# The opening stage of a hybrid encoder step: norm_pre behind the transposes for two tiles, POOL and DVE shares moved, a written order of squares and splits

## The chip, the core and the metric

The kernel runs on one core of a Trainium2 chip. The core has five engines with instruction streams of their own: TensorE (PE in the profile; its weight loads are listed as PEld), VectorE (DVE), ScalarE (ACT), GpSimd (POOL) and SyncE (SP, which here only issues DMAs). The metric is the device time of one execution in microseconds (us); lower is better. The time before is 2414.46 us, the median of three runs (2413.88 to 2417.59).

## The reference

One layer of a streaming encoder: RMSNorm, one combined input projection, two groups of attention heads, per-head norms and gates, one output projection, and a second RMSNorm. It is computed for 1024 prompt frames and for 8 x 16 sample frames (128 rows). What matters for the change is the start:

```python
def rms_norm(x, g):
    xf = x.astype(jnp.float32)
    y = xf * lax.rsqrt(jnp.mean(xf * xf, axis=-1, keepdims=True) + EPS)
    return (y * g.astype(jnp.float32)).astype(x.dtype)

...
    h = rms_norm(xp, norm_pre[l])
    q_sb, k_sb, v_sb, gate_sb, q_r, k_r, v_r, gate_r = project(h, w_in[l], pos_p)
```

`x` has 2048 columns, `w_in` is 2048 x 8192, all in float32. `rms_norm` multiplies each row by a number of its own (1/rms) and each column by `norm_pre`.

## The kernel before

The frames are tiles of 128 rows. Group 0 holds the prompt tiles 0 to 3 and the sample tile (the "tile 4" of the text, loaded as `x_sample`), group 1 the prompt tiles 4 to 7. For the projections the normalised `h` must lie transposed (its 2048 columns on partitions, as 16 blocks of 128) and as two float32r parts whose sum is `h`: the high part `mh` and the low part `ml`. A product is then three matmuls: high by high, low by high, high by low. The weights are split in the same way (`wr` into `wh` and `wl`).

The opening stage brings group 0 into that form. For a tile it does this:

- SP loads the rows, `xt`, 128 x 2048 (`load_x`, line 355).
- ACT squares the row and adds it up (`sq`, line 361); ACT and DVE make 1/rms of it (`inv_rms`, lines 137 to 143: `p0v`, `p0r`, `p0u`, six operations on 128x1 of which three have two inputs in SBUF).
- DVE multiplies the identity by 1/rms, row by row: the diagonal matrix `dg` (line 388).
- `xt` is multiplied by `norm_pre` in place, in eight pieces of 256 columns (line 391): on DVE for tile 0 and tile 4, on POOL for the tiles 1 to 3. `gpre` is `norm_pre` copied to all 128 partitions by two DMAs of 512 KB.
- PE multiplies each block of `xt` by `dg`, which transposes and scales it at once (line 371), four blocks (a quarter) to a PSUM buffer `p0t`, of which there are four. Tile 4 is scaled on DVE instead (line 395) and transposed with the identity (line 369).
- ACT copies the quarter into `mh` (line 129) and DVE subtracts for `ml` (line 130).

After tile 1 the first weight column (`load_w`: four chunks, each loaded, split and multiplied) is applied to the 256 columns of tiles 0 and 1 (`products`, line 226, into the first bank of `acc`); after tile 4 to the other 384 columns (second bank). Then come the projection of the next column (again line 226) and `project_rows` (line 285, into `accn`), which is the first work of PE in which the two kernels do not differ any more. Beside these products a background job (`stage_rest`) loads, squares, scales (line 428 on DVE, 128x2048) and transposes the tiles of group 1.

A scheduler sets the order of instructions on each engine when the program is built; the source gives it dependencies, and here and there an order only (`tc.add_manual_dep` with SCHED_ONLY, `tc.issue_after`). Each engine then runs its stream in that order, and an instruction that waits holds up those behind it.

## Time and profile before

| what | value |
|---|---|
| median of 3 runs | 2414.46 us |
| the profiled execution | 2413.81 us, span 2412.1 us |
| PE busy over the span | 2338.0 us (97%) |
| DVE, ACT, POOL busy over the span | 1255.4, 913.6, 647.9 us |
| DVE `ml` from PSUM, 128x512 | 20 by 678 ns |
| ACT square of a tile, 128x2048 | 9 by 1909 ns |
| POOL multiply by `gpre`, 128x256 | 24 by 824 ns |

All times of the trace are from the start of the span. In a row of the timeline stand the start, the time to the end of the last instruction, the engine, the line of the source, the operation, its tiles (written <- read) and its count; in brackets how long the engine had been idle and what ended that. A mean or a busy time of PE is no measure of its speed, since its matmuls overlap; the distance from start to start is. Clock means the share of PE's full clock that was granted. Lines are those of the kernel before; in the kernel after the same operations have other line numbers.

### The profile page before, as it was taken

Reading aid. Unit: us, or ns where it says so; the run is one execution under the profiler, and the core shown is the slowest. Engines: PE = TensorE matmul, PEld = TensorE weight load, DVE = VectorE, ACT = ScalarE, POOL = GpSimd, SP = SyncE. Lnnn points to the kernel's source line nnn. Section 1 sums busy time; section 2 is a strip of 40 time slices with the busy share of each in tenths; the row PEclk is TensorE's granted clock in tenths of the full one; section 3 lists DMA queues with packets and bytes.
Section 4 is the critical chain, followed back from the end, with each engine's and each line's share of the span. In section 5 each row is a group of like instructions: output and inputs, shape, how many; then the busy total and the mean of one; then the engine's idle time right before and its main releaser. Section 6 shows DMA issues by size and latency. Waiting matters only on the chain.

```text
span 2412.1 us, 40463 instructions
## 1 busy us (share of the span) xinstructions
PE 2338.0 (97%) x14832; PEld 2099.1 (87%) x14832; DVE 1255.4 (52%) x2434; ACT 913.6 (38%) x1929; POOL 647.9 (27%) x1029
## 2 busy tenths in 40 slices
PE   7999999999999999998999999999999998999998
PEld 7998999999999999997778888889888877878787
DVE  7245445455554555455545555554545564564544
ACT  6323333333333333324333334333443343444343
POOL 3144353444444353443202112120120211000000
PEclk9999999999999999999999999999999999999999
DMA  7669779797978788797965565665556566765554
GB/s 243 167 129 218 157 172 195 174 199 160 197 170 189 174 180 189 186 190 186 198 169 146 140 158 152 148 146 153 139 150 152 154 167 165 233 210 182 190 183 130
DMA packets 674888, 418.67 MB, mean 174 GB/s; under 512 B 224512, under 2 KB 619776, under 8 KB 672256
## 3 DMA queue, kind: packets, MB, share of 16 engines
q1 hardware_dynamic: 524272, 285.99, 48.3%
q0 software_dynamic: 32256, 71.36, 13.5%
q10 hardware_dynamic: 118160, 58.74, 8.8%
q8 instruction: 116, 1.90, 0.3%
q14 instruction: 84, 0.69, 0.1%
HBM read 336.24 MB, written 79.69 MB: 172 GB/s over the span
## 4 chain that ended last, share of the span: by engine, by line
PE 84%; DMA 8%; DVE 4%; ACT 1%; issue 1%; POOL 1%; SPq 0%; DVEq 0%; ACTq 0%; POOLq 0%
PE acc L226 45%; PE accn L285 17%; PE a L993 3%; PE a L994 3%; PE a L992 3%; DMA mr<-s_y 3%; PE pa L615 3%; PE z L585 2%; DMA wr<-w_in 2%; PE zc L658 1%; PE pd L725 1%; DMA wr<-w_out 1%; DVE ml L130 1%; DVE out L1054 1%; DVE wl L130 1%
## 5 line engine op out<-in xcount | busy, mean ns | idle before, releaser
L226 PE MATMUL acc<-mh,wh 128*128 128x256 f32 (+2 forms) x2304 | 664.0, 341 | 6.4 <-ACT wh L129 4.7
L226 PE MATMUL acc<-ml,wh 128*128 128x384 f32 (+2 forms) x2304 | 665.4, 342 | 0.0
L226 PE MATMUL acc<-mh,wl 128*128 128x256 f32 (+2 forms) x2304 | 659.2, 339 | 0.9 <-DVE wl L130 0.7
L130 DVE TENSOR_TENSOR wl<-wr,wh 128x512 fp32r<-128x512 f32 (+1 forms) x576 | 393.4, 688 | 504.6 <-ACT wh L129 502.3
L129 ACT ACTIVATE wh<-wr 128x512 fp32r<-128x512 f32 (+1 forms) x576 | 356.1, 624 | 685.4 <-PE acc L226 255.0
L226 PEld LDWEIGHTS acc<-mh,wh 128*128 128x128 f32 x2304 | 420.8, 189 | 41.9 <-ACT wh L129 5.6
L226 PEld LDWEIGHTS acc<-ml,wh 128*128 128x128 f32 x2304 | 422.6, 189 | 33.4 <-issue 6.2
L226 PEld LDWEIGHTS acc<-mh,wl 128*128 128x128 f32 x2304 | 424.2, 189 | 31.0 <-DVE wl L130 2.6
L642 POOL DMA_DIRECT2D kc<-cache_sb_k x512 | 331.3, 653 | 366.2 <-DVE kcT L680 201.5
L285 PE MATMUL accn<-whn,mh 128*128 128x256 f32 x1152 | 330.1, 287 | 2.7 <-DVE rg L312 2.7
L285 PE MATMUL accn<-wln,mh 128*128 128x256 f32 x1152 | 326.8, 284 | 2.2 <-DVE wln L130 2.2
L285 PE MATMUL accn<-whn,ml 128*128 128x256 f32 x1152 | 326.6, 284 | 0.0
L285 PEld LDWEIGHTS accn<-whn,mh 128*128 128x128 f32 x1152 | 221.3, 192 | 12.3 <-issue 7.7
L993 PE MATMUL a<-wl,mh 128*128 128x512 f32 (+1 forms) x576 | 221.6, 385 | 7.1 <-DVE wl L130 7.0
L285 PEld LDWEIGHTS accn<-wln,mh 128*128 128x128 f32 x1152 | 221.8, 193 | 2.8 <-DVE wln L130 2.4
L285 PEld LDWEIGHTS accn<-whn,ml 128*128 128x128 f32 x1152 | 221.6, 192 | 0.0
L992 PE MATMUL a<-wh,mh 128*128 128x512 f32 (+1 forms) x576 | 219.9, 384 | 0.8 <-DVE so L618 0.5
L994 PE MATMUL a<-wh,ml 128*128 128x512 f32 (+1 forms) x576 | 220.6, 383 | 0.0
L993 PEld LDWEIGHTS a<-wl,mh 128*128 128x128 f32 x576 | 109.4, 190 | 29.8 <-DVE wl L130 9.0
L130 DVE TENSOR_TENSOR wln<-wrn,whn 128x512 fp32r<-128x512 f32 x128 | 86.7, 688 | 88.9 <-ACT whn L129 88.9
L478 POOL DMA_DIRECT2D be<-s_be x128 | 94.1, 741 | 131.0 <-DMA s_be<-be 116.5
L503 POOL TENSOR_SCALAR_AFFINE_SELECT kp<-kp 128x128 f32<-128x128 f32 x40 | 14.5, 362 | 426.0 <-ACT kp L497 425.9
(189 smaller groups left out, 2680.5 us busy)
## 6 DMA issues: line engine op xcount, KB each, us to landing
wr<-w_in SPq DMA_DIRECT2D x384, 256.0 KB, 4.2
wr<-w_out SPq DMA_DIRECT2D x184, 256.0 KB, 3.6
wrn<-w_in SPq DMA_DIRECT2D x128, 256.0 KB, 3.2
kc<-cache_sb_k POOLq DMA_DIRECT2D x512, 64.0 KB, 5.1
vc<-cache_sb_v SPq DMA_DIRECT2D x64, 512.0 KB, 9.1
xt<-x_prompt SPq DMA_DIRECT2D x8, 1024.0 KB, 6.0
xr<-x_prompt SPq DMA_DIRECT2D x8, 1024.0 KB, 6.5
out<-out ACTq DMA_DIRECT2D x12, 512.0 KB, 2.9
```

Of the source, the lines that this page charges most:

```text
L129: nc.scalar.activation(hi, src, AF.Copy)
L130: nc.vector.tensor_tensor(lo, src, hi.bitcast(F32), ALU.subtract)
L226: last = nc.tensor.matmul(a[:, :m], lhs[:, j, :], rhs[w][:, j, o : o + m], start=(w == 0 and j == 0 and n == 0), stop=(w == KT // WQ - 1 a ...
L285: anchor[0] = nc.tensor.matmul(a, lhs[q][:, jj, ts], rhs[:, j, :], start=(w == 0 and j == 0 and n == 0 and t % 2 == 0), stop=(w == KT // 2 ...
L478: q.dma_start(raw[32 * i : 32 * i + 32, :].rearrange("p (k a) -> p k a", a=32), s[:, :, 32 * i : 32 * i + 32].rearrange("k (j b) a -> b (k ...
L585: nc.tensor.matmul(z[:, :c], q2[a][:, i * P : (i + 1) * P], k2[b][:, s : s + c], start=(m == 0), stop=(m == 2),)
L615: nc.tensor.matmul(po[:, :P], at[:, j, :], vn[:, j, :], start=(j == 0), stop=(j == t))
L642: nc.gpsimd.dma_start(kc[32 * i : 32 * i + 32, :].rearrange("p (k d) -> p k d", d=32), cache_k[0, 2 * c + j, s * 512 : (s + 1) * 512, h, 3 ...
L658: mm = nc.tensor.matmul(z[r, :], qp[:, j, r], ready[2 * j + c // 2][:, c % 2, :], start=(j == 0), stop=(j == 1),)
L992: nc.tensor.matmul(a[:, :width], hi[q][:, j, ts], wh, start=(k == 0), stop=False)
L993: nc.tensor.matmul(a[:, :width], hi[q][:, j, ts], wl, start=False, stop=False)
L994: nc.tensor.matmul(a[:, :width], lo[q][:, j, ts], wh, start=False, stop=(k == KT - 1))
```

## The change

- Tiles 0 and 1 are no longer multiplied by `norm_pre` before the transposes. `norm_pre` is also loaded as 16 rows of 128 (`grow`, on ACT's DMA queue), transposed by PE and copied to `gcol`, 128x16. After a transpose the columns of `x` lie on partitions, so `gcol` is a factor per partition: DVE multiplies the quarter out of PSUM by it into an SBUF tile `xg`, and the split reads `xg`.
- The low parts of the first six quarters (all of tile 0, two of tile 1) are subtracted on POOL, the other two of tile 1 on DVE.
- The tiles 2 and 3 are still multiplied by `gpre` on POOL, tile 4 on DVE. Tile 4 gets a `dg` as well, and no scaling on DVE.
- PE starts with twenty matmuls of a constant tile (`busy`), whose results nobody reads.
- `x` of tile 1 is loaded ahead of `gpre`.
- Squares, multiplies, weight splits and the first transposes of a tile are told not to be placed ahead of named instructions of PE. Tile 4's second to fourth quarter are transposed between the products of the second bank, a quarter ahead of each fourth of the products.

```diff
+        low.tensor_tensor(lo, src, hi.bitcast(F32), ALU.subtract)
...
-            loaded = [load_x(tiles[0])]
+            busy = p0s.tile([P, P], F32, name="busy")
+            nc.vector.memset(busy, 1.37)
+            grow = p0s.tile([KT, P], F32, name="grow")
+            nc.scalar.dma_start(grow, norm_pre[0].rearrange("(k p) -> k p", p=P))
+            loaded = [load_x(tiles[0]), load_x(tiles[1])]
+            pt = p0p.tile([P, 4, P], F32, name="p0t", tag="p0t")
+            for j in range(WARM):
+                nc.tensor.matmul(pt[:, j % 4, :], busy, busy, start=True, stop=True)
...
+            gcol = p0s.tile([P, KT], F32, name="gcol")
+            pt = p0p.tile([P, 4, P], F32, name="p0t", tag="p0t")
+            nc.tensor.transpose(pt[:, 0, :KT], grow, ident[:KT, :KT])
+            nc.vector.tensor_copy(gcol, pt[:, 0, :KT])
...
+            def stats(i, other=None):
+                with tc.high_priority():
+                    rstd = mean_square(loaded[i], other)
                     dg = p0.tile([P, P], F32, name="dg", tag="dg")
                     nc.vector.tensor_scalar(dg, ident, rstd, None, ALU.mult)
-                for c in range(PRE_CUT):
...
+                for c in range(8 if i > 1 else 0):
+                    cs = slice(c * D // 8, (c + 1) * D // 8)
+                    eng = nc.gpsimd if i < 4 else nc.vector
+                    ins = eng.tensor_tensor(loaded[i][:, cs], loaded[i][:, cs], gpre[:, cs], ALU.mult)
+                    behind(ins, other)
...
+            def turn_quarter(i, q, dg, other=None):
+                cs = slice(i * P, (i + 1) * P)
+                pt = turn(q, loaded[i], dg, other)
+                hi, lo = mov[0][q][:, :, cs], mov[1][q][:, :, cs]
+                if i > 1:
+                    split(hi, lo, pt)
+                    return
+                xg = p0.tile([P, 4, P], F32, name="xg", tag="xg", bufs=3)
+                nc.vector.tensor_tensor(
+                    xg, pt, gcol[:, 4 * q : 4 * q + 4].unsqueeze(2).to_broadcast([P, 4, P]), ALU.mult
+                )
+                split(hi, lo, xg, None, nc.gpsimd if 4 * i + q < 6 else nc.vector)
+
+            scales = [stats(0), stats(1)]
+            for q in quarters:
+                turn_quarter(0, q, scales[0])
+            raw = [fetch_w(col(4, 0), q) for q in quarters]
+            loaded += [load_x(t) for t in tiles[2:]]
+            w4 = []
+            for q in quarters:
+                turn_quarter(1, q, scales[1])
+                w4.append((q, *split_w(raw[q], anchor[0])))
+            scales.append(stats(2, anchor[0]))
+            acc = acc_banks(g0)
+            for n, w in enumerate(w4):
+                last = products(mov, acc[:1], g0["pieces"][:1], *w)
+                if n == 1:
+                    scales.append(stats(3, last))
+            for i in (2, 3):
+                for q in quarters:
+                    turn_quarter(i, q, scales[i], last if q == 0 else None)
+                if i == 2:
+                    scales.append(stats(4, anchor[0]))
+            for q in quarters:
+                turn_quarter(4, q, scales[4], last if q else None)
+                last = products(mov, acc[1:], g0["pieces"][1:], *w4[q])
```

What this makes of the order shows on three engines. POOL, from its start to its first cache loads (`kc`), before; `ident` is the identity, and the count at the end is that of equal instructions:

```order
masks.py:197 MEMSET ident 128x128
masks.py:199 ISA
masks.py:199 AFFINE_SELECT ident<-ident 128x128
L391 TENSOR_TENSOR xt<-xt,gpre 128x256 x24
L642 DMA kc<-cache_sb_k 32x16x32 x29
```

The same place of POOL after; `ml_142` to `ml_148` are the low parts of the four quarters, first of tile 0, then of tile 1:

```order
L134 TENSOR_TENSOR ml_142<-xg,mh_141 128x4x128
L134 TENSOR_TENSOR ml_144<-xg,mh_143 128x4x128
L134 TENSOR_TENSOR ml_146<-xg,mh_145 128x4x128
L134 TENSOR_TENSOR ml_148<-xg,mh_147 128x4x128
L134 TENSOR_TENSOR ml_142<-xg,mh_141 128x4x128
L134 TENSOR_TENSOR ml_144<-xg,mh_143 128x4x128
L421 TENSOR_TENSOR xt<-xt,gpre 128x256 x16
```

Tile 1's eight multiplies are gone from POOL; six subtractions of twice the width stand ahead of the sixteen multiplies of tiles 2 and 3.

DVE before, where the low parts of tile 3 (the first `ml_142` to `ml_148` here) and of tile 4 (the second set) are made; `sw` and `rq` belong to the first product bank, L395 is tile 4's scaling:

```order
L391 TENSOR_TENSOR xt<-xt,gpre 128x256 x2
L130 TENSOR_TENSOR ml_142<-p0t,mh_141 128x4x128
L395 TENSOR_SCALAR xt<-xt,p0r 128x2048
L321 TENSOR_TENSOR sw<-sw,sinT 128x256
L322 TENSOR_TENSOR rq<-acc_322,cosT 128x256
L130 TENSOR_TENSOR ml_144<-p0t,mh_143 128x4x128
L130 TENSOR_TENSOR ml_146<-p0t,mh_145 128x4x128
L130 TENSOR_TENSOR ml_148<-p0t,mh_147 128x4x128
L130 TENSOR_TENSOR ml_142<-p0t,mh_141 128x4x128
L130 TENSOR_TENSOR ml_144<-p0t,mh_143 128x4x128
```

The same place of DVE after; the L421 row is the last of tile 4's eight multiplies, and the second `ml_142` is the first subtraction of tile 4:

```order
L417 TENSOR_SCALAR dg<-ident,p0r 128x128
L421 TENSOR_TENSOR xt<-xt,gpre 128x256 x2
L134 TENSOR_TENSOR ml_142<-p0t,mh_141 128x4x128
L134 TENSOR_TENSOR ml_144<-p0t,mh_143 128x4x128
L134 TENSOR_TENSOR ml_146<-p0t,mh_145 128x4x128
L134 TENSOR_TENSOR ml_148<-p0t,mh_147 128x4x128
L134 TENSOR_TENSOR ml_142<-p0t,mh_141 128x4x128
```

And what follows there, up to the second subtraction of tile 4; L478 is the scaling of a tile of group 1 (L428 before):

```order
L141 TENSOR_SCALAR p0v<-ssq 128x1
L143 RECIPROCAL p0r<-p0r 128x1
L144 TENSOR_TENSOR p0u<-p0r 128x1
L145 TENSOR_TENSOR p0u<-p0u,p0v 128x1
L146 TENSOR_SCALAR p0u<-p0u 128x1
L147 TENSOR_TENSOR p0r<-p0r,p0u 128x1
L478 SCALAR_TENSOR_TENSOR xt<-xt,p0r,gpre 128x2048
L141 TENSOR_SCALAR p0v<-ssq 128x1
L134 TENSOR_TENSOR ml_144<-p0t,mh_143 128x4x128
```

All eight multiplies of tile 4 now stand ahead of tile 3's four subtractions, and between the first and the second subtraction of tile 4 stand a scale chain and a scaling of group 1.

PE before, from the end of the first product bank (`acc_322`) to the start of the second (`acc_323`):

```order
L226 MATMUL acc_322<-mh_147,wl 128x256
L371 MATMUL p0t<-dg,xt 128x128 x32
L369 MATMUL p0t<-ident,xt 128x128 x8
L226 MATMUL acc_323<-mh_141,wh 128x384
L369 MATMUL p0t<-ident,xt 128x128 x8
L226 MATMUL acc_323<-ml_142,wh 128x384
```

PE after, some rows on, between the first and the second fourth of the second bank (now `acc_352`; `acc_599` and `acc_600` are the two banks of the next weight column):

```order
L235 MATMUL acc_352<-ml_142,wh 128x384
L235 MATMUL acc_352<-mh_141,wl 128x384
L389 MATMUL p0t<-dg,xt 128x128 x4
L235 MATMUL acc_352<-mh_143,wh 128x384
L235 MATMUL acc_599<-mh_141,wh 128x256
L235 MATMUL acc_600<-mh_141,wh 128x384
L235 MATMUL acc_352<-ml_144,wh 128x384
```

Tile 4's quarters moved in between the products, as float32 matmuls by `dg` and no longer as transposes with the identity.

More of the change, by code (lines that the diff above doesn't have):

```diff
@@ L27 @@
 WQ = 4
-PRE_POOL = (1, 2, 3)
-PRE_DIAG = (0, 1, 2, 3)
-PRE_CUT = 8
-PRE_G = 2
 D_REST = 8
+WARM = 20
 KC_AHEAD = 2
@@ L126, in tile_hybrid_step, with split @@
     ]
-    def split(hi, lo, src):
-        nc.scalar.activation(hi, src, AF.Copy)
-        nc.vector.tensor_tensor(lo, src, hi.bitcast(F32), ALU.subtract)
+    def split(hi, lo, src, behind=None, low=nc.vector):
+        ins = nc.scalar.activation(hi, src, AF.Copy)
+        if behind is not None:
+            tc.add_manual_dep(
+                ins.ins,
+                behind.ins.name,
+                mybir.DependencyInfo(mybir.DependencyClass.NoSync, mybir.DependencyReason.SCHED_ONLY),
+                reason="not placed ahead of the transposes",
+            )
+        low.tensor_tensor(lo, src, hi.bitcast(F32), ALU.subtract)
     def inv_rms(pool, ssq, n, name):
@@ L370, in turn @@
                     else:
-                        nc.tensor.matmul(pt[:, j, :], blk, scale, start=True, stop=True)
+                        anchor[0] = nc.tensor.matmul(pt[:, j, :], blk, scale, start=True, stop=True)
+                        if j == 0:
+                            behind(anchor[0], other)
                 return pt
             tiles = g0["tiles"]
-            loaded = [load_x(tiles[0])]
+            busy = p0s.tile([P, P], F32, name="busy")
+            nc.vector.memset(busy, 1.37)
@@ L402, in tile_hybrid_step @@
+                return dg
+            def turn_quarter(i, q, dg, other=None):
                 cs = slice(i * P, (i + 1) * P)
-                for q in range(KT // 4):
-                    pt = turn(q, loaded[i], scales[i])
-                    split(mov[0][q][:, :, cs], mov[1][q][:, :, cs], pt)
-                if i == 1:
-                    w4 = list(load_w(col(4, 0)))
-                    loaded += [load_x(t) for t in tiles[3:]]
-                    acc = acc_banks(g0)
-                    for w in w4:
-                        products(mov, acc[:1], g0["pieces"][:1], *w)
@@ L412, in tile_hybrid_step @@
-            for w in w4:
-                last = products(mov, acc[1:], g0["pieces"][1:], *w)
+                pt = turn(q, loaded[i], dg, other)
[6 more added lines that the diff above has]
+                    xg, pt, gcol[:, 4 * q : 4 * q + 4].unsqueeze(2).to_broadcast([P, 4, P]), ALU.mult
+                )
```

58 lines of the change are left out of this document (27 added, 31 removed).

## The prediction

> **What bounds the kernel now.** I read the page's busy line and chain first, to see which engine a microsecond has to be taken from.
>
> ```profile
> PE 2338.0 (97%) x14832; PEld 2099.1 (87%) x14832; DVE 1255.4 (52%) x2434; ACT 913.6 (38%) x1929; POOL 647.9 (27%) x1029
> ...
> PE 84%; DMA 8%; DVE 4%; ACT 1%; issue 1%; POOL 1%; SPq 0%; DVEq 0%; ACTq 0%; POOLq 0%
> ```
>
> TensorE (PE) is the bound, so a change in the opening stage is worth what it changes in PE's waiting and in PE's own work there. The second view, the waits of the first 45 us, says where PE waits today (and POOL, in the first row); the columns are the total, how often, and the longest.
>
> ```profile
> POOL xt L391 <- ACT sq L361: 13.7, 2, 12.3
> PE p0t L371 <- DVE dg L388: 10.6, 1, 10.6
> ...
> PE p0t L371 <- DVE p0v L137: 2.2, 1, 2.2
> ...
> PE p0t L371 <- issue: 1.5, 1, 1.5
> ...
> PE p0t L369 <- DVE xt L395: 1.0, 1, 1.0
> ...
> PE p0t L369 <- DVE ml L130: 0.5, 1, 0.5
> ```
>
> Third, PE in order of time. A start is followed by the time to the last end. One fp32 matmul is two passes, so a tile's sixteen are "x32"; the transposes of the sample tile with the identity are one pass each (x4 a quarter).
>
> ```profile
> 10.56 6.05 PE L371 MATMUL p0t<-dg,xt 128*128 128x128 f32 x32 [10.56 <-DVE dg L388]
> 18.84 5.35 PE L371 MATMUL p0t<-dg,xt 128*128 128x128 f32 x32 [2.22 <-DVE p0v L137]
> 23.94 0.36 PE L226 MATMUL acc<-mh,wh 128*128 128x256 f32 x1
> ...
> 30.39 3.74 PE L371 MATMUL p0t<-dg,xt 128*128 128x128 f32 x32
> 35.66 3.81 PE L371 MATMUL p0t<-dg,xt 128*128 128x128 f32 x32 [1.53 <-issue]
> 40.42 0.63 PE L369 MATMUL p0t<-ident,xt 128*128 128x128 f32 x4 [0.96 <-DVE xt L395]
> 41.59 0.66 PE L369 MATMUL p0t<-ident,xt 128*128 128x128 f32 x4 [0.55 <-DVE ml L130]
> 42.01 0.43 PE L226 MATMUL acc<-mh,wh 128*128 128x384 f32 x1
> 42.27 1.18 PE L369 MATMUL p0t<-ident,xt 128*128 128x128 f32 x8
> 43.39 0.44 PE L226 MATMUL acc<-ml,wh 128*128 128x384 f32 x1
> ...
> 67.53 0.28 PE L285 MATMUL accn<-whn,mh 128*128 128x256 f32 x1
> ```
>
> From 43.39 PE is fed without a gap. My yardstick is the last row: the first L285 product at 67.53. Behind it every engine has the same instructions in the same order before and after the change, so what that row moves by, the end moves by.
>
> Fourth, the clock. The columns are the stretch, its length, busy time of PE, PEld, DVE, ACT, POOL, and the granted clock.
>
> ```profile
> 10.00:15.00 5.00, 4.44 (x21) 4.44 (x22) 2.09 (x7) 3.17 (x5) 1.35 (x2) 1.00 1.05 381
> ...
> 15.20:18.60 3.40, 1.42 (x12) 1.22 (x11) 2.68 (x8) 2.84 (x4) 3.40 (x6) 1.00 1.14 368
> 18.60:22.10 3.50, 3.26 (x15) 3.29 (x16) 2.84 (x6) 1.91 (x5) 3.50 (x5) 0.51 0.99 399
> ```
>
> A stretch in which PE worked 1.42 of 3.40 us is followed by one at half clock. A pass is 0.211 us at the slow rate (4.44/21) and 0.117 at the full one (3.74/32).
>
> **The change, step by step.** I follow PE and keep account of its lead over the kernel before.
>
> *Tile 0.* Its scale `dg` no longer shares VectorE (DVE) with eight multiplies.
>
> ```profile
> 5.76 1.91 ACT L361 ACTIVATE sq<-xt 128x2048 f32<-128x2048 f32 x1 [3.45 <-DMA xt<-x_prompt]
> ...
> 8.22 0.16 DVE L139 RECIPROCAL p0r<-p0r 128x1 f32<-128x1 f32 x1
> ...
> 10.23 0.28 DVE L388 TENSOR_SCALAR dg<-ident,p0r 128x128 f32<-128x128 f32 x1
> ...
> 11.57 1.91 ACT L361 ACTIVATE sq<-xt 128x2048 f32<-128x2048 f32 x1 [3.38 <-DMA xt<-x_prompt]
> ...
> 29.07 0.16 DVE L139 RECIPROCAL p0r<-p0r 128x1 f32<-128x1 f32 x1 [0.27 <-ACT p0r L138]
> 29.27 0.16 DVE L140 TENSOR_TENSOR p0u<-p0r 128x1 f32<-128x1 f32 x1
> 29.47 0.59 DVE L141 TENSOR_TENSOR p0u<-p0u,p0v 128x1 f32<-128x1 f32 x1
> ...
> 30.28 0.47 DVE L143 TENSOR_TENSOR p0r<-p0r,p0u 128x1 f32<-128x1 f32 x1
> 30.79 0.72 DVE L388 TENSOR_SCALAR dg<-ident,p0r 128x128 f32<-128x128 f32 x1
> ```
>
> Undisturbed steps follow each other by 0.20 us (29.07 to 29.27). From the reciprocal at 8.22 that is four steps, a 0.15 copy of `gcol`, and the 0.28 of `dg`: ready at 9.45 and not 10.51. The twenty warm matmuls are 40 passes, 4.7 to 8.4 us from about 1.2 us on, inside PE's first wait of 10.6: they cost nothing. With the clock up the tile takes 3.74 and not 6.05: done at 13.3, before at 16.6. **Lead 3.3** (1.1 if the clock is not up).
>
> *Tile 1.* Its load is issued ahead of the 1 MB of `gpre`; at the 381 GB/s above that brings its square from 11.57 to about 8.9. But its scale chain now runs while POOL does the low-part subtractions of tile 0. In the rows at 29.47, 30.28 and 30.79, three steps that cost 0.16, 0.16 and 0.28 alone took 0.59, 0.47 and 0.72 beside POOL's multiplies. POOL's instructions:
>
> ```profile
> 13.65 11.94 POOL L391 TENSOR_TENSOR xt<-xt,gpre 128x256 f32<-128x256 f32 x16 [12.28 <-ACT sq L361]
> ...
> 27.01 6.85 POOL L391 TENSOR_TENSOR xt<-xt,gpre 128x256 f32<-128x256 f32 x8 [1.43 <-ACT sq L361]
> ```
>
> ```profile
> L391 POOL TENSOR_TENSOR xt<-xt,gpre 128x256 f32<-128x256 f32 x24 | 18.8, 824 | 13.7 <-ACT sq L361 13.7
> ...
> L1052 POOL TENSOR_TENSOR out<-out,xr 128x512 f32<-128x512 f32 x3 | 5.2, 1738 | 120.8 <-ACT out L1051 120.8
> ```
>
> A 128x512 subtraction is not in the trace on POOL: two multiplies of 11.94/16 give 1.49, the 128x512 addition gives 1.74; I take 1.45, since the low end is the same operation on the same engine. A DVE step caught behind one waits about twice what it waited behind a multiply: four steps lose 2 to 4 us, three 0.69 multiplies by `gcol` stand between them, and from the step at 11.1 `dg` comes at about 16.4 (14.5 to 17.5). Transposes from 16.4, not 18.84; after 3.1 us of idling I charge the half clock again (5.35, as before): done at 21.8 against 24.2. **Lead 2.4.** The 48 products follow as they do now (6.4 us): **lead 2.0** at their end, 28.3.
>
> [...]
>
> *Tile 2 and 3.* This is where I see the lead go. POOL now has six subtractions (about 8.7 us) ahead of the sixteen multiplies; the fifth and sixth wait for tile 1's transposes (18 to 20) plus its `gcol` multiply and split, so POOL is through at about 23. Then it waits for ACT's square of tile 2, which is held behind tile 1's transposes and stands behind four weight splits: 22.9 to 25. Eight multiplies at 6.85 (the row at 27.01): tile 2 is multiplied at 31.8, before at 25.6. PE finishes tile 2 at about 33.0, before at 34.1: **lead 1.1**. Eight more, 6.0 to 6.85: tile 3 is multiplied at 38.2, before at 33.86. PE waits 2.5 us and finishes tile 3 at about 40, before at 39.47: **behind by 0.5**.
>
> *Tile 4.* It loses the 1.2 us scaling (L395), but keeps its eight multiplies on DVE, and these now stand ahead of the four subtractions of tile 3.
>
> ```profile
> L130 DVE TENSOR_TENSOR ml<-p0t,mh 128x512 fp32r<-128x512 f32 x20 | 13.0, 678 | 2.5 <-ACT mh L129 2.3
> L428 DVE SCALAR_TENSOR_TENSOR xt<-xt,p0r,gpre 128x2048 f32<-128x2048 f32 x4 | 9.4, 2349 | 0.0
> L391 DVE TENSOR_TENSOR xt<-xt,gpre 128x256 f32<-128x256 f32 x16 | 7.8, 506 | 0.0
> ```
>
> From about 36.4, eight multiplies at 0.506, one subtraction and the scale's steps last until 41.6. The first quarter of tile 4 needs the PSUM buffer that the next subtraction frees, at 42.2. Eight passes (0.9 to 1.7), ACT's split (0.6), DVE's (0.68): the second product, the one that needs the low part, starts at 44.6 to 45.5, before at 43.39. **Behind by 1.7** (1.2 to 2.1).
>
> *From there to the yardstick.* Before: 67.53 - 43.39 = 24.1 us of uninterrupted PE. After, the three other quarters of tile 4 come between the products, 24 passes by 0.117 = 2.8 us of added work. For the second quarter PE waits: transposes, split and subtraction are in series, and DVE has a 2.35 us L428 operation ahead of the subtraction. I charge 1.5 (0.6 to 2.5), since products of the next column fill the later quarters. For the half clock after the idling at 37 to 42 I charge 1.0 (0 to 2).
>
> **Sum:** 1.7 + 2.8 + 1.5 + 1.0 = 7.0 us later at 67.53. The profiled execution took 2413.81 (span 2412.1); 2420.8. The median of the runs, 2414.46, lies 0.65 above it: I say **2421**. The low ends give 1.2 + 2.8 + 0.6 + 0 = 4.6, less 1.4 if the blocks stay short; the high ends 9.4, and about 2 more if a subtraction costs 1.74.
>
> [...]
>
> **The rivals.** 0.2% is 4.8 us, about what a measurement of this kernel tells from no change.
>
> *The lead is kept (faster).* If POOL finishes tile 3 by about 33 and not 38, PE runs into tile 4 without waiting. Then the 3.3 of tile 0 stays, the waits of 1.5, 1.0 and 0.5 go, and 16 extra passes cost 1.9: -4.4, so 2410. It decides at POOL's first multiply: it must start near 20, not 25. For it: DVE loses eight multiplies and a scaling. Against it: POOL is busy without a break from 13.65 to 25.6 now, and gets 8.7 us of subtractions for the 6 us of multiplies that it loses, with a later start. 0.10.
>
> *The loss is covered (no change).* Tile 3 is late as said, but the waits at tile 4's quarters are filled by products and the clock stays up: 1.2 + 2.8, some 4 us less what overlaps; 2417. For it: the program does place products of the next column between the quarters. 0.20.
>
> *POOL costs more.* At 1.74 a subtraction, with multiplies and DVE's weight splits blocked more often, tile 2 and 3 slip by another 3 to 5 us: 2425 to 2428. 0.10.
>
> **How the numbers follow.** The forecast, 4.8 to 10 us later, has 0.60. Of the faster case 0.06 lies beyond 0.2%; the rest of it and the covered case make 0.24; forecast and last rival 0.70. The range 2415 to 2426 leaves out the faster case and the worse half of the last one.
>
> **What the profile after would show.** Right: PE's first transposes near 9.5 at the full rate; tile 1's near 16.4; POOL's first multiply near 25 and its last ending near 38; a PE wait before tile 3's last quarter; the first L285 product near 74.5. Wrong: multiplies on POOL that start by 21, small DVE steps of 0.16 us beside the subtractions, a first L285 product at or before 67.5, or an end that does not move with that row.

## The result and the profile after

The kernel after takes 2423.78 us (median of 7 runs, 2420.46 to 2429.24); the kernel before, run beside it, 2414.46. The ratio is 1.0038, with a 95% interval of 1.0027 to 1.005: 9.2 us slower, between 6.5 and 12.1. The same program was timed again later with the experiments (E12 below): 1.0031 (1.0017 to 1.0045), 7.5 us. The profiled execution took 2427.99 us (span 2426.3), near the slow end of its runs.

First PE in order of time, the view that answers to the third one of the prediction. The columns are the same; L389 is the transposes, L235 the products, L294 the first work that both kernels share.

```profile
10.03 3.84 PE L389 MATMUL p0t<-dg,xt 128*128 128x128 f32 x32 [2.18 <-DVE dg L417]
17.01 3.81 PE L389 MATMUL p0t<-dg,xt 128*128 128x128 f32 x32 [3.14 <-issue]
20.57 0.36 PE L235 MATMUL acc<-mh,wh 128*128 128x256 f32 x1
...
38.01 1.13 PE L389 MATMUL p0t<-dg,xt 128*128 128x128 f32 x8 [2.05 <-DVE p0u L144]
41.00 2.08 PE L389 MATMUL p0t<-dg,xt 128*128 128x128 f32 x8 [1.85 <-DVE ml L134]
43.76 0.69 PE L235 MATMUL acc<-mh,wh 128*128 128x384 f32 x1 [0.69 <-ACT mh L126]
44.49 0.69 PE L235 MATMUL acc<-ml,wh 128*128 128x384 f32 x1
44.97 0.52 PE L235 MATMUL acc<-mh,wl 128*128 128x384 f32 x1
45.29 0.52 PE L235 MATMUL acc<-mh,wh 128*128 128x384 f32 x1
...
48.17 1.61 PE L389 MATMUL p0t<-dg,xt 128*128 128x128 f32 x8
50.47 1.09 PE L235 MATMUL acc<-mh,wh 128*128 128x384 f32 x3 [0.69 <-ACT mh L126]
...
51.57 0.33 PE L235 MATMUL acc<-mh,wl 128*128 128x384 f32 x1
51.74 0.34 PE L235 MATMUL acc<-mh,wh 128*128 128x384 f32 x1
...
53.33 1.05 PE L389 MATMUL p0t<-dg,xt 128*128 128x128 f32 x8
54.14 0.54 PE L235 MATMUL acc<-ml,wh 128*128 128x256 f32 x2
...
75.37 0.28 PE L294 MATMUL accn<-whn,mh 128*128 128x256 f32 x1
```

The yardstick, the last row, stands at 75.37 and not at 67.53: the opening loses **7.84 us**. PE is 3.4 us ahead of the kernel before at its first product (20.57 against 23.94), waits 2.05 and 1.85 us at tile 3's last quarter and at tile 4's first, and is 1.1 us behind at the second product of the second bank (44.49 against 43.39). The other 6.7 us are lost from there on. The clock by stretch says how; the columns are the stretch, its length, the busy time of PE, PEld, DVE, ACT and POOL, the granted clock, and two of the DMAs.

```profile
36.00:41.00 5.00, 1.13 (x9) 0.97 (x9) 5.00 (x17) 3.06 (x5) 0.93 (x2) 0.81 0.45 138
41.00:43.70 2.70, 2.08 (x8) 1.78 (x8) 1.74 (x3) 1.25 (x3) 0.00 (x0) 0.50 0.82 340
43.70:48.10 4.40, 4.30 (x12) 3.90 (x13) 3.92 (x9) 2.10 (x4) 0.00 (x0) 0.50 0.00 0
```

In the five microseconds from 36 on PE works 1.13; the granted clock falls within them (0.81 on the mean), and from 41 to past 48 it is half. The products of 384 columns then follow each other by 0.32 us (44.97 to 45.29) and not by 0.17, as later at full clock (51.57 to 51.74).

POOL and DVE, which set the waits, in order of time, and POOL's subtractions as a group (busy time, mean ns of one, idle before them):

```profile
12.66 3.91 POOL L134 TENSOR_TENSOR ml<-xg,mh 128x512 fp32r<-128x512 f32 x3 [11.29 <-ACT p0r L142]
16.73 1.31 POOL L134 TENSOR_TENSOR ml<-xg,mh 128x512 fp32r<-128x512 f32 x1 [0.16 <-ACT mh L126]
19.68 2.99 POOL L134 TENSOR_TENSOR ml<-xg,mh 128x512 fp32r<-128x512 f32 x2 [1.64 <-ACT mh L126]
24.74 12.18 POOL L421 TENSOR_TENSOR xt<-xt,gpre 128x256 f32<-128x256 f32 x16 [2.08 <-ACT sq L379]
...
12.92 1.04 DVE L144 TENSOR_TENSOR p0u<-p0r 128x1 f32<-128x1 f32 x1
...
20.05 1.46 DVE L134 TENSOR_TENSOR wl<-wr,wh 128x512 fp32r<-128x512 f32 x1
...
35.46 1.74 DVE L421 TENSOR_TENSOR xt<-xt,gpre 128x256 f32<-128x256 f32 x2
...
37.20 0.67 DVE L134 TENSOR_TENSOR ml<-p0t,mh 128x512 fp32r<-128x512 f32 x1
```

```profile
L134 POOL TENSOR_TENSOR ml<-xg,mh 128x512 fp32r<-128x512 f32 x6 | 8.1, 1360 | 13.2 <-ACT p0r L142 11.3 <-ACT mh L126 1.8
```

Beside POOL's subtractions a DVE step that costs 0.16 alone takes 1.04, and a weight split of 0.68 takes 1.46. Then POOL's sixteen multiplies follow, from 24.74 to 36.92. The wait of 2.05 us ends after them: PE starts at 38.01, when DVE has made the last low part of tile 2 (37.20 to 37.87) and so freed a PSUM buffer. That subtraction stood behind two of DVE's multiplies of tile 4, which took 0.87 each beside POOL's.

Of the 14.2 us by which the profiled execution is longer, 7.84 are made in the opening. The rest is scatter: E12, another execution of the same program, is without it.

### The profile page after: what moved, and what is told of

It reads as the page before. It is cut to its first block, busy times and chain, and to the rows that moved or that the text cites. A ratio compares the mean times of both kernels' runs of the same rounds, so it can differ in the third digit from the quotient of the medians.

```text
span 2426.3 us, 40574 instructions
## 1 busy us (share of the span) xinstructions
PE 2352.0 (97%) x14889; PEld 2107.0 (87%) x14889; DVE 1258.7 (52%) x2430; ACT 914.6 (38%) x1929; POOL 651.4 (27%) x1027
## 4 chain that ended last, share of the span: by engine, by line
PE 77%; DMA 11%; DVE 4%; issue 4%; ACT 2%; POOL 1%; SPq 1%; ACTq 0%; DVEq 0%; POOLq 0%
PE acc L235 39%; PE accn L294 17%; PE a L1043 4%; PE a L1044 4%; PE a L1042 4%; DMA mr<-s_y 3%; DMA wr<-w_in 3%; PE pa L665 2%; PE z L635 2%; PE zc L708 1%; DMA s_rk<-rk 1%; DMA kb<-s_be 1%; PE pd L775 1%; DMA ro<-s_rk 1%; SPq L528 1%
## 5 line engine op out<-in xcount | busy, mean ns | idle before, releaser
L235 PE MATMUL acc<-mh,wh 128*128 128x256 f32 (+2 forms) x2304 | 665.3, 342 | 8.2 <-ACT wh L126 6.0
L235 PE MATMUL acc<-ml,wh 128*128 128x384 f32 (+2 forms) x2304 | 666.8, 342 | 0.2
L235 PE MATMUL acc<-mh,wl 128*128 128x256 f32 (+2 forms) x2304 | 660.0, 340 | 0.6 <-DVE wl L134 0.2
L235 PEld LDWEIGHTS acc<-mh,wh 128*128 128x128 f32 x2304 | 421.5, 189 | 45.4 <-ACT wh L126 7.6
L235 PEld LDWEIGHTS acc<-ml,wh 128*128 128x128 f32 x2304 | 423.5, 189 | 34.8 <-issue 6.2
L235 PEld LDWEIGHTS acc<-mh,wl 128*128 128x128 f32 x2304 | 425.0, 189 | 30.7 <-issue 2.1
L294 PE MATMUL accn<-whn,mh 128*128 128x256 f32 x1152 | 329.7, 287 | 2.8 <-DVE rg L321 2.0
L294 PE MATMUL accn<-wln,mh 128*128 128x256 f32 x1152 | 326.5, 284 | 2.7 <-DVE wln L134 2.7
L294 PE MATMUL accn<-whn,ml 128*128 128x256 f32 x1152 | 326.0, 283 | 0.0
L294 PEld LDWEIGHTS accn<-whn,mh 128*128 128x128 f32 x1152 | 220.9, 192 | 12.6 <-issue 7.7
L294 PEld LDWEIGHTS accn<-wln,mh 128*128 128x128 f32 x1152 | 221.4, 192 | 3.8 <-DVE wln L134 3.4
L294 PEld LDWEIGHTS accn<-whn,ml 128*128 128x128 f32 x1152 | 221.2, 192 | 0.0
```

Of the source, the lines that this page charges most:

```text
L235: last = nc.tensor.matmul(a[:, :m], lhs[:, j, :], rhs[w][:, j, o : o + m], start=(w == 0 and j == 0 and n == 0), stop=(w == KT // WQ - 1 a ...
L294: anchor[0] = nc.tensor.matmul(a, lhs[q][:, jj, ts], rhs[:, j, :], start=(w == 0 and j == 0 and n == 0 and t % 2 == 0), stop=(w == KT // 2 ...
```

## The experiments

All are compared at the yardstick, the first product of `project_rows`, in one profiled execution each, and by their time against the kernel before on the same chip.

| | yardstick | against before | time by the ratio | 95% interval |
|---|---|---|---|---|
| before | 67.53 | | | |
| after | 75.37 | +7.84 | +9.2 | 6.5 to 12.1 |
| E12, after again | 76.15 | +8.62 | +7.5 | 4.1 to 10.9 |
| E1, after, quarters first | 72.30 | +4.77 | +4.6 | 1.7 to 7.5 |
| E2, after, subtractions on DVE | 73.11 | +5.58 | +9.7 | 5.8 to 13.5 |
| E3, after, tile 2 early | 76.16 | +8.63 | +11.1 | 7.2 to 15.0 |
| E4, after, one warm matmul | 73.08 | +5.55 | +6.8 | 4.3 to 9.2 |
| E5, before with warm matmuls | 66.73 | -0.80 | -2.4 | -5.3 to 0.5 |
| E6, after, tile 4 on POOL | 72.77 | +5.24 | +10.6 | 7.5 to 13.5 |
| E7, E1 with plain tile 4 | 71.18 | +3.65 | +4.3 | 1.7 to 7.0 |
| E8, scale in the split | 65.20 | -2.33 | -3.6 | -6.0 to -1.2 |
| E9, before, interleaved | 71.29 | +3.76 | +5.6 | 2.9 to 8.0 |
| E10, E1 and E2 together | 69.97 | +2.44 | +3.1 | 0.7 to 5.8 |
| E11, E8 with weights first | 64.35 | -3.18 | -1.7 | -4.8 to 1.4 |

The fourth column is the ratio less one, times 2414.46. The two columns agree but for E2 (by a little) and E6. Each yardstick is that of one execution, and the two of the kernel after differ by 0.78 us, so a difference of that size shows nothing by itself. One thing that varies is the clock at tile 1: its 32 passes took 3.81 us in the first profiled execution of the kernel after, in E4 and in E6, 5.44 in E1, E2, E7 and E10, and more than 6.5 in E3 and E12.

**E1: tile 4's quarters ahead of the second bank.**

```diff
             for q in quarters:
-                turn_quarter(4, q, scales[4], last if q else None)
+                turn_quarter(4, q, scales[4])
+            for q in quarters:
                 last = products(mov, acc[1:], g0["pieces"][1:], *w4[q])
```

> The kernel after, with one edit: all four quarters of tile 4 are transposed ahead of the products of the second bank, and not one ahead of each fourth of them. The yardstick is the first product of project_rows: 67.53 us before, 75.36 after. Theory A (the prediction's: a large part of the loss is made by the quarters between the products, which wait for a split and a subtraction each while the clock is down): the two waits of 0.69 us go, and the products between 43.7 and 50 run at the normal pitch; the yardstick comes at 71 to 73, the time is 2 to 4 us shorter than that of the kernel after. The 24 added passes (2.8 us) stay, so it remains slower than the kernel before by 4 to 6. Rival B (the quarters only wait for tile 3, which is late anyway; where they stand makes no difference): yardstick within 0.7 us of 75.36.

The yardstick moves by 3.07 us to 72.30, as theory A said. The wait for tile 4 and the half clock stay; they now meet the 32 passes and not the products:

```profile
41.53 6.74 PE L389 MATMUL p0t<-dg,xt 128*128 128x128 f32 x32 [1.85 <-DVE ml L134]
```

That is 0.21 us a pass; at 0.117 these would be 3.74 us, and the half clock costs 3.0 here too. What E1 removes is the series of transposition, split and subtraction between the products.

**E9: the interleaving alone, put into the kernel before.**

```diff
                 for q in range(KT // 4):
-                    pt = turn(q, loaded[i], scales[i])
+                    with tc.issue_after(last.ins) if i == 4 and q else nullcontext():
+                        pt = turn(q, loaded[i], scales[i])
                     split(mov[0][q][:, :, cs], mov[1][q][:, :, cs], pt)
+                    if i == 4:
+                        last = products(mov, acc[1:], g0["pieces"][1:], *w4[q])
...
-            for w in w4:
-                last = products(mov, acc[1:], g0["pieces"][1:], *w)
```

> The kernel before, with one edit: tile 4's quarters are transposed one ahead of each fourth of the second-bank products, as the kernel after does, and nothing else of it (tile 4 stays scaled on DVE and transposed with the identity, one pass a block). Theory A (the interleaving costs by itself, since each fourth of the products waits for a transposition, a split and a subtraction in series, and DVE has a 2.35 us operation ahead of one): PE waits 0.5 to 2 us in two places behind 42 us, yardstick 69.5 to 71.5 (67.53 before), time 2 to 4 us above the kernel before. Rival J (it costs only where tile 3 is late and the clock is down, as in the kernel after; with tile 3 in time, products of the next column fill the gaps): yardstick 67 to 68.5.

71.29: the interleaving costs 3.76 us without anything else of the change, with tile 3 in time and with one pass a block. PE in order of time, and the clock:

```profile
41.74 0.45 PE L226 MATMUL acc<-mh,wh 128*128 128x384 f32 x1 [0.69 <-ACT mh L129]
43.40 0.44 PE L226 MATMUL acc<-ml,wh 128*128 128x384 f32 x1 [1.21 <-DVE ml L130]
43.68 0.36 PE L226 MATMUL acc<-mh,wl 128*128 128x384 f32 x1
43.85 0.50 PE L226 MATMUL acc<-mh,wh 128*128 128x384 f32 x1
44.16 0.52 PE L226 MATMUL acc<-ml,wh 128*128 128x384 f32 x1
```

```profile
40.00:43.40 3.40, 1.07 (x6) 0.61 (x6) 3.40 (x8) 3.08 (x5) 0.00 (x0) 1.00 0.82 275
43.40:46.80 3.40, 3.40 (x12) 3.30 (x13) 0.40 (x3) 0.34 (x3) 0.00 (x0) 0.57 0.08 34
```

In the kernel before, the other quarters' transposes fill PE's waits for the first quarter's split and subtraction (42.27 to 43.39). Held behind the products they can't: PE waits 0.69 and 1.21 us, works 1.07 us in 3.4, and the products behind that run at a clock of 0.57 over the next 3.4. Theory A holds, rival J falls.

**E2: all low parts on DVE.**

```diff
-                split(hi, lo, xg, None, nc.gpsimd if 4 * i + q < 6 else nc.vector)
+                split(hi, lo, xg, None, nc.vector)
```

> The kernel after, with one edit: the low parts of the first six quarters are subtracted on DVE and not on POOL. POOL is left with the sixteen multiplies of tiles 2 and 3. Theory A (POOL's six subtractions make tiles 2 and 3 late): small DVE steps take 0.16 us again between 12 and 22; POOL's first multiply starts at 21 to 23 (24.74 after) and its last ends at 35 or earlier (36.92); yardstick 73 to 74. Rival C (the square of tile 2, placed behind tile 1's transposes and four weight splits, decides, not the subtractions): POOL's first multiply still starts at 24 to 25; yardstick within 0.7 us of 75.36. Rival D (DVE is the full engine, so that six more subtractions on it cost as much as they free): the first-bank products end later than 27.8, and the yardstick is at 75 or later.

73.11: 2.26 us gained. The small DVE steps are short again and POOL starts 1.9 us earlier (the view puts its wait down to a DMA; ACT's square of tile 2 had ended at 22.79, just before):

```profile
13.41 0.15 DVE L144 TENSOR_TENSOR p0u<-p0r 128x1 f32<-128x1 f32 x1
...
18.44 0.68 DVE L134 TENSOR_TENSOR wl<-wr,wh 128x512 fp32r<-128x512 f32 x1
...
22.88 13.12 POOL L421 TENSOR_TENSOR xt<-xt,gpre 128x256 f32<-128x256 f32 x16 [21.50 <-DMA xt<-x_sample]
```

Theory A holds in size at the yardstick. Part of rival D is in it as well: the last product of the first bank starts at 29.51 and not at 27.51. The timed ratio shows no gain over the kernel after; its interval (5.8 to 13.5) begins just above what the yardstick gives (5.58).

**E10: E1 and E2 together.**

> The kernel after with both edits of E1 and E2: tile 4's quarters ahead of the second bank, and all subtractions on DVE. E1 gained 3.07 us at the yardstick and E2 2.26. If the two causes are separate (interleaving in one place, POOL's subtractions in another): 75.37 - 5.3 = 70.0, within 0.8. If they overlap (a late tile 3 is paid for once): 71.3 to 72.3. Either way it stays behind the kernel before (67.53) by the 24 added passes, about 2.8, if these are on the path.

69.97, a gain of 5.40 where the sum of the two was 5.33: the causes are separate (that the two figures agree to 0.07 is chance, given the scatter of 0.78). The time agrees: 3.1 us above the kernel before. The 2.44 us that are left are there by the start of the second bank: its second product begins at 45.93, 2.54 later than in the kernel before, behind 32 passes for tile 4 that still begin after a wait of 1.85 us and run partly at half clock (0.70 granted on the mean from 40.40 to 46.00).

```profile
40.45 5.47 PE L389 MATMUL p0t<-dg,xt 128*128 128x128 f32 x32 [1.85 <-DVE ml L134]
```

**E7: E1, and tile 4 scaled on DVE and transposed with the identity.**

```diff
-                    dg = p0.tile([P, P], F32, name="dg", tag="dg")
-                    nc.vector.tensor_scalar(dg, ident, rstd, None, ALU.mult)
+                    dg = p0.tile([P, P], F32, name="dg", tag="dg") if i < 4 else None
+                    if i < 4:
+                        nc.vector.tensor_scalar(dg, ident, rstd, None, ALU.mult)
...
+                if i == 4:
+                    nc.vector.tensor_scalar(loaded[4], loaded[4], rstd, None, ALU.mult)
```

> As E1 (all quarters of tile 4 ahead of the second bank), and tile 4 is also scaled on DVE and transposed with the identity, as in the kernel before: one pass a block and not two. Against E1 (yardstick 72.30) PE has 16 passes less (1.9 us at 0.117) and DVE has 1.2 us more. Theory A (PE's added passes are on the path): yardstick 70.2 to 71.2. Rival H (DVE is on the path, its 1.2 us of scaling takes the place of what PE saves): yardstick 71.7 to 73.

71.18, 1.12 less than E1: PE's passes are on the path (A), but DVE's scaling eats a part of it: tile 4's first quarter begins at 42.59 after a wait of 2.94 us, in E1 at 41.53 after 1.85. So the second pass of tile 4 costs 1.1 us net and not 1.9. That is not far above the scatter of 0.78, and the time does not show it (4.3 against 4.6).

**E6: tile 4's multiplies on POOL.**

```diff
-                    eng = nc.gpsimd if i < 4 else nc.vector
+                    eng = nc.gpsimd
```

> The kernel after, with tile 4's eight multiplies by gpre on POOL behind those of tile 3, and not on DVE. Theory A2 (DVE's multiplies of tile 4 stand ahead of tile 3's subtractions, and so hold up the PSUM buffers that PE needs at 38.01 and 41.00): the wait of 2.05 us ahead of tile 3's last quarter falls below 1, the first second-bank product comes at 41.5 to 43 instead of 43.76, yardstick 73 to 74.2. Rival G (POOL is late anyway, and with eight more multiplies, 5.5 to 6 us, tile 4 is later still): POOL's last multiply ends at 42.5 to 44, tile 4's first quarter starts at or after 42.5, yardstick 75.4 to 78.

At the yardstick 72.77, a gain of 2.60, a little more than theory A2 said: the wait ahead of tile 3's last quarter is 0.33 us, not 2.05, and in its place stands a longer one ahead of tile 4.

```profile
36.01 1.23 PE L389 MATMUL p0t<-dg,xt 128*128 128x128 f32 x8 [0.33 <-DVE p0r L143]
40.24 2.05 PE L389 MATMUL p0t<-dg,xt 128*128 128x128 f32 x8 [3.00 <-DVE p0v L141]
```

The time does not follow: 10.6 us slower than before, as slow as the kernel after. The profiled execution of E6 was the shortest of its ten. What its other executions lose, and where, is open.

**E3: tile 2 early.**

```diff
+            loaded += [load_x(tiles[2])]
+            scales.append(stats(2))
             raw = [fetch_w(col(4, 0), q) for q in quarters]
-            loaded += [load_x(t) for t in tiles[2:]]
+            loaded += [load_x(t) for t in tiles[3:]]
...
-            scales.append(stats(2, anchor[0]))
```

> The kernel after, with tile 2 brought forward: its load is issued ahead of the four weight chunks, and its square is no longer held behind tile 1's transposes. The subtractions stay on POOL. Rival C (the held square is what makes tiles 2 and 3 late): POOL's first multiply starts at 17 to 19 and not at 24.74, tile 3 is multiplied by 33 and not by 36.92, the wait of 2.05 us ahead of tile 3's last quarter goes, yardstick 72 to 73.5. Theory E (DVE and POOL are one resource here, since each blocks the other when both read SBUF twice; an early multiply is paid for by the splits beside it): POOL's multiplies do start at 18, but the first-bank products end at 32 to 34 instead of 27.8, and the yardstick is at 75 to 78: not better, or worse.

76.16: nothing gained, although POOL starts on tile 2 at 18.16 as planned. POOL, DVE, and PE's first product with a low part of tile 1:

```profile
18.16 5.97 POOL L421 TENSOR_TENSOR xt<-xt,gpre 128x256 f32<-128x256 f32 x8 [0.59 <-ACT sq L379]
24.09 2.51 POOL L134 TENSOR_TENSOR ml<-xg,mh 128x512 fp32r<-128x512 f32 x2
27.67 6.98 POOL L421 TENSOR_TENSOR xt<-xt,gpre 128x256 f32<-128x256 f32 x8 [1.07 <-ACT sq L379]
...
24.18 1.19 DVE L145 TENSOR_TENSOR p0u<-p0u,p0v 128x1 f32<-128x1 f32 x1
25.41 0.15 DVE L146 TENSOR_SCALAR p0u<-p0u 128x1 f32<-128x1 f32 x1
25.49 1.66 DVE L134 TENSOR_TENSOR wl<-wr,wh 128x512 fp32r<-128x512 f32 x1
...
25.41 0.39 PE L235 MATMUL acc<-ml,wh 128*128 128x256 f32 x1 [2.21 <-POOL ml L134]
```

Two of tile 1's low parts now stand behind the multiplies on POOL and PE waits 2.21 us for them, DVE's splits for the first bank run into them (1.66 and not 0.68), and the last product of the first bank starts at 33.34 (27.51 after). Theory E's yardstick and bank end came; what goes earlier on POOL is paid for elsewhere. That the blocking between DVE and POOL is the whole reason is not shown: the wait of 2.21 us comes from POOL's own order, and tile 1 ran at half clock in this execution (DVE's `xg` for its first three quarters began at 18.70, 20.41 and 22.11, about 0.21 us a pass), so that the first product came at 22.84 and not at 20.57. Rival C's yardstick did not come, but its first steps did: tile 3 was multiplied by 34.65, and the wait ahead of its last quarter shrank to 0.61. Since the edit itself delays the first bank, this run can't say what the held square alone costs.

**E4 and E5: the warm matmuls.** E4 is the kernel after with one of them, E5 the kernel before with twenty.

```diff
-            for j in range(WARM):
-                nc.tensor.matmul(pt[:, j % 4, :], busy, busy, start=True, stop=True)
+            nc.tensor.matmul(pt[:, 0, :], busy, busy, start=True, stop=True)
```

> The kernel after, with one matmul of the constant tile instead of twenty. Theory A (the warm matmuls bring the clock up for tile 0 and cost nothing): tile 0's 32 passes take about 6 us at half clock, not 3.84, tile 0 ends at 16 and not at 13.6; 2.3 us of lead go there, and the yardstick is at 75.4 to 77.5. Rival F (tile 0's transposes are ahead of what DVE and POOL can use, so their speed does not reach the end): tile 0 ends at 16, yet the yardstick stays within 1 us of 75.36, or is earlier.

```diff
             tiles = g0["tiles"]
+            busy = p0s.tile([P, P], F32, name="busy")
+            nc.vector.memset(busy, 1.37)
+            pt = p0p.tile([P, 4, P], F32, name="p0t", tag="p0t")
+            for j in range(WARM):
+                nc.tensor.matmul(pt[:, j % 4, :], busy, busy, start=True, stop=True)
```

> The kernel before, with only the twenty matmuls of a constant tile ahead of the first transposes. Theory A (a faster tile 0 is a lead that PE keeps): tile 0's transposes take about 3.8 us instead of 6.05, and the yardstick moves from 67.53 to 65.3. Rival F (tile 0 is ahead of what DVE and POOL can use; E4 spoke for it): tile 0 ends 2.2 us earlier, tile 1's transposes still start at 18.5 to 19.5, since POOL's multiplies of tile 1 end there, and the yardstick stays at 67 to 68.6.

PE's first rows, E4's and then E5's:

```profile
9.66 5.62 PE L389 MATMUL p0t<-dg,xt 128*128 128x128 f32 x32 [5.40 <-DVE dg L416]
16.36 3.81 PE L389 MATMUL p0t<-dg,xt 128*128 128x128 f32 x32 [1.09 <-issue]
```

```profile
10.56 3.84 PE L372 MATMUL p0t<-dg,xt 128*128 128x128 f32 x32 [2.65 <-DVE dg L394]
18.82 5.44 PE L372 MATMUL p0t<-dg,xt 128*128 128x128 f32 x32 [4.42 <-DVE p0v L138]
```

In E4 tile 0 ends 1.4 us later, and yet the yardstick is 2.29 earlier. In E5 tile 0 ends 2.2 us earlier, tile 1 starts when it did (18.82, before 18.84), and the yardstick gains 0.80: a little more than rival F allowed, far less than theory A's 2.2, and no more than the scatter. Rival F holds in the main: the later tiles do not wait for tile 0. E4 also changed the order of steps on DVE and ACT (tile 1's scale comes ahead of some `gcol` multiplies), since the scheduler plans with the matmuls that it sees; its gain is that order's or the clock's, which this run can't tell apart.

**E8 and E11: a version that takes work off DVE and POOL.** E8 is the kernel before with the warm matmuls, tile 1 loaded ahead of `gpre`, and `gcol` for the tiles 0 and 1 inside the split; the core of it:

```diff
+                    if i in PRE_GCOL:
+                        hi, lo = mov[0][q][:, :, cs], mov[1][q][:, :, cs]
+                        for j in range(4):
+                            k = 4 * q + j
+                            nc.scalar.activation(hi[:, j, :], pt[:, j, :], AF.Copy, scale=gcol[:, k : k + 1])
+                        for j in range(4):
+                            k = 4 * q + j
+                            nc.vector.scalar_tensor_tensor(
+                                lo[:, j, :], pt[:, j, :], gcol[:, k : k + 1], hi[:, j, :].bitcast(F32),
+                                ALU.mult, ALU.subtract,
+                            )
+                        continue
```

> A kernel built on theory E: take the work of norm_pre off DVE and POOL. It is the kernel before with the warm matmuls, x of tile 1 ahead of gpre, and gcol for tiles 0 and 1, but without xg: ACT makes the high part straight from PSUM with gcol as its scale (four 128x128 a quarter), and DVE makes the low part in one operation, PSUM times gcol minus the high part (four 128x128 a quarter). Tiles 2 and 3 are multiplied on POOL, tile 4 on DVE with the identity, as before. Theory E (DVE with POOL is the full resource of the stage): DVE spends less on tiles 0 and 1 than in either kernel (eight quarters at about 1.0, and neither 16 multiplies nor POOL's blocks), POOL starts tile 2 at 15 to 18 and has tile 3 multiplied by 30 to 31, the second bank starts at 37.5 to 39.5, yardstick 62.5 to 64.5, time 3 to 5 us below the kernel before. Rival I (the small operations cost ACT and DVE too much: 32 each, with a fixed cost): yardstick 66 to 69, time within 2 us of the kernel before.

65.20 and 2413.9 us against 2415.82: ratio 0.9985 (0.9975 to 0.9995). It is the one kernel whose interval lies below 1; the ratio stands for 3.6 us. What the warm matmuls alone have in that was not taken apart: E5, which has only them, is at -2.4 (-5.3 to 0.5), and at 0.80 of the 2.33 us at the yardstick. The yardstick missed the expected 62.5 to 64.5 by 0.7: tile 2's transposes got in among the first products, waited 3.36 us for POOL and ran at half clock (0.50 granted from 21.70 to 25.20).

```profile
21.76 2.47 PE L373 MATMUL p0t<-dg,xt 128*128 128x128 f32 x10 [3.36 <-POOL xt L404]
...
24.46 4.00 PE L373 MATMUL p0t<-dg,xt 128*128 128x128 f32 x20
```

E11 puts them behind the first bank and loads the weights ahead of tile 2:

```diff
-            loaded += [load_x(t) for t in tiles[2:3]]
...
             for i, t in enumerate(tiles):
+                if i == 1:
+                    w4 = list(load_w(col(4, 0)))
+                    loaded.append(load_x(tiles[2]))
...
-                    pt = turn(q, loaded[i], scales[i])
+                    with tc.issue_after(last.ins) if i == 2 and q == 0 else nullcontext():
+                        pt = turn(q, loaded[i], scales[i])
...
-                        products(mov, acc[:1], g0["pieces"][:1], *w)
+                        last = products(mov, acc[:1], g0["pieces"][:1], *w)
```

> E8 with two changes of order: the four weight chunks are loaded ahead of tile 2's rows, and tile 2's first transposes are placed behind the first-bank products. In E8 these transposes stood in the midst of the products, waited 3.36 us for POOL and ran at half clock. If that is what E8 lost against its expectation: the first product comes at 16 to 18 (23.89 in E8), PE waits less than 1 us at a time until 25, tile 2's wait of 2.5 us comes later (31 to 34), yardstick 63 to 64.5 (65.20). If the stage is held by DVE and ACT in any order: yardstick 65 to 66.5, time as E8 within 1 us.

The yardstick is 64.35, and the first product starts at 17.57 (23.89 in E8). That agrees with the expectation that E8 lost by its order, though the 0.85 us gained are hardly more than the scatter. The time, 2413.9 against 2416.3, ratio 0.9993 (0.998 to 1.0006), does not show the further gain.

**E12: the kernel after again.**

> The kernel after, unchanged, for the scatter: how far the yardstick and the part behind it differ between two profiled executions of one program. If the opening is set by its program, the yardstick comes within 1 us of 75.37; the part behind it, which was 6.4 us longer than in the profiled execution of the kernel before, then shows by how much single executions differ there: if that part is scatter it is shorter by several us this time, if it belongs to the change it is again 6 to 7 us longer.

The yardstick is 76.15, 0.78 later. The part behind it is 2344.6 us of the span; it was 2350.9 in the first profiled execution and 2344.6 in that of the kernel before. So those 6.4 us were scatter. Tile 1 ran at half clock this time (0.50 granted from 16 to 20 us, 1.00 in the first execution):

```profile
9.71 3.84 PE L389 MATMUL p0t<-dg,xt 128*128 128x128 f32 x32 [1.48 <-DVE dg L417]
16.68 6.63 PE L389 MATMUL p0t<-dg,xt 128*128 128x128 f32 x31 [3.13 <-issue]
```

## Why the prediction was right, step by step

The forecast was 7 us later; it became 7.84 and 8.62 at the yardstick, 9.2 and 7.5 in the measured time. Four of its steps held, the last of them in size only:

- Tile 0 at full rate: predicted from 9.5, done at 13.3; measured from 10.03, done at 13.87 (the load came 0.4 later).
- Tile 1's scale slowed by POOL's subtractions: transposes predicted at 16.4, measured at 17.01. No run shows the 1.4 us that the range takes off if the blocks stay short, which were my estimate. In the kernel after the three steps that met a subtraction took 1.04, 0.70 and 0.68 us, where one costs 0.16 alone; beside POOL's multiplies, in the kernel before, two such steps took 0.59 and 0.47.
- POOL's first multiply predicted at 25, measured at 24.74; end 38.2 against 36.92. The subtraction cost 1.36 on the mean (8.1 us for six), not 1.45.
- The wait ahead of tile 3's last quarter (2.5 predicted, 2.05), and the second product of the second bank at 44.6 to 45.5 (44.49). Behind there: 1.1, not 1.7. The reason for the wait was only half right. The prediction let POOL's last multiply end it, at 38.2. POOL was through at 36.92, which accounts for 0.96 of the 2.05; the rest is DVE's subtraction for tile 2, behind two multiplies of tile 4. In E6, where these multiplies are gone from DVE, the wait is 0.33. The prediction counted these multiplies against tile 4's first quarter, where they do cost a wait (1.85), but not here.

Three were off:

- The terms behind that point. I had 2.8 for passes, 1.5 for waits and 1.0 for the half clock, 5.3 in all; it is 6.74 (30.88 from the second product to the yardstick, before 24.14). The half clock costs 2.3: eleven products in 3.68 us that take 1.9 at the pitch of 0.173, and eight passes in 1.61 that take 1.05 later on (the row at 53.33). Passes cost 2.7 (1.05, then twice 0.81 from start to start), the one wait 0.69; the other 1.0 lies in short gaps between transposes and products, for which the sum had no term. **The term that was mis-sized is the half clock**, which I took at 1.0 with a bound of 2. That the total came within a microsecond is in part luck: the start of the second bank (0.6) and the wait (0.8) were taken too high, the half clock (1.3) and the gaps (1.0) too low.
- Tile 1 at half clock, which I charged in full. In one execution it did not come, in the other it did. The first products of the two differ by 2.6 us (20.57 and 23.18), the yardsticks by 0.78.
- The lead. I let PE's 3.3 us at tile 0 stand as something that PE keeps until DVE and POOL use it up. E5 gives at most 0.80 for 2.2 us of it and E4 less than nothing: tiles 1 to 3 are paced by DVE and POOL, not by when tile 0 is out. The *lead is kept* rival counted it in full, so by E5 its 2410 was too good a price for that case.

*The loss is covered* did not come: products of the next column filled the waits at tile 4's third and fourth quarter, but not the one at the second (0.69), and the clock did not stay up (0.50 from 41 to past 48). The interleaving cost 3.1 (E1) to 3.8 us (E9) by itself. *POOL costs more* did not come, as the subtractions were cheaper than assumed. The causes, by the experiments and at the yardstick: the interleaving 3.1 to 3.8, POOL's subtractions 2.3, the sum of both 5.4, tile 4's second pass 1.1 net. If E7's step is taken off the 2.44 that E10 leaves, some 1.3 remain, which were not taken apart; DVE's multiplies of tile 4 ahead of tile 3's subtractions are the likely place (E6's 2.6 at the yardstick), but E6's time leaves that open.

That the end moves with the yardstick held for the medians, but for E2 and E6, and not for one execution: behind it, the profiled executions of these kernels scatter between 2342 and 2351 us.

## What to carry to other kernels

Work that is moved from a full engine to an idle one can still hold the full one up: here DVE steps of 0.16 us took up to 1.04 beside POOL's six subtractions, and these, moved back to DVE, gave 2.3 us at the yardstick. Starting POOL's multiplies earlier gained nothing where other work of POOL then stood behind them. Transposes that could fill PE's wait for a split should not be held behind the products that need it; in E9 the wait was paid twice, once as itself (0.69 and 1.21 us) and once as a clock of 0.57 over the 3.4 us behind it. Before a lead on the bounding engine is counted, look for who paces the next step: 2.2 us at tile 0 were worth less than one.

## What the runs showed of the hardware

- The same program, with the same idling ahead of tile 1 (3.14 and 3.13 us), kept its full clock in one execution (1.00 granted from 16 to 20 us, 32 passes in 3.81) and fell to half in the other (0.50, 31 passes in 6.63). And in E9 waits of 0.69 and 1.21 us, with 1.07 us of work in 3.4, were followed by a clock of 0.57 over the next 3.4. What decides whether the clock falls is not shown.
- The prediction read tile 0's 0.211 us a pass as the slow rate, although its clock row for 10 to 15 us says 1.00. E5 bears the pitch out: behind twenty warm matmuls the same 32 passes take 3.84 us and not 6.05.
- POOL's 128x512 subtraction took 1.36 us on the mean. DVE instructions with two SBUF inputs that met it lost up to most of its length (0.16 became 1.04 in the kernel after, 0.68 became 1.66 in E3), while one with a PSUM input did not (`xg`, eight by 0.685 on the mean, 0.68 to 0.69 beside POOL's subtractions too). It went the other way as well: POOL's subtraction that began at 20.91, beside DVE's weight split of 20.05 to 21.51, took 1.75, where the median of the six is 1.28.
- ACT's split of 128x512 from PSUM takes 0.60 us; as four pieces of 128x128 with a scale per partition it takes 1.06 (sixteen in 4.25 in E8). DVE's low part, multiplied and subtracted in four such pieces, takes 1.06 (fourteen in 3.71).
